# Inverse square roots by one power on GpSimd, and eight weight subtractions moved to VectorE

## The chip, the core and the metric

The kernel runs on one core of a Trainium2 chip. The metric is the time of one execution on the device in microseconds; the time before is the median of three runs.

## What is computed

One inference step of a layer with two kinds of mixer. 512 prompt tokens and 8 sequences of 4 new ("sample") tokens, 1,024 wide, are RMS-normalised and multiplied by one input matrix. Its columns are q and k (4 heads, each twice 64), v (4 x 128), and u and a gate input (512 each) of a gated MLP. Everything that matters here is where an inverse square root stands:

```python
def rms_norm(x, g):
    y = x * lax.rsqrt(jnp.mean(x * x, axis=-1, keepdims=True) + EPS)
    return y * g

z  = rms_norm(x, norm_mix) @ w_in
q  = rms_norm(z[q columns] per head half, q_gain)        # k the same
gv = rms_norm(gelu(z[gate columns]) per group, gv_gain)
mix = gelu(z[u columns]) * (W_s gv + b)                  # W_s lower triangular, 128 x 128
att = softmax(q1 k1) v - lam * softmax(q2 k2) v          # causal; sample tokens also read 4,096 cached rows
h   = x + [rms_norm(att, subln_gain) * 0.8, mix] @ w_out
out = h + relu(rms_norm(h, norm_ffn) @ w_up)**2 @ w_down
```

The outputs are y, k and v for both kinds of token and the sample's gv.

## The kernel before

Exact float32 products are made from split operands: every weight tile of 128 x 1,024 that is loaded (`raw`) is copied by ScalarE into `wh` (float32r), and the rest `raw - wh` goes into `wl`; TensorE then multiplies hi by hi, lo by hi and hi by lo. `w_conv()` does this split. Its subtraction runs on VectorE, except that of weight tiles 12 to 19, which runs on GpSimd:

```python
(G if 12 <= i < 20 else V).tensor_tensor(out=lo, in0=raw, in1=hi, op=ALU.subtract)
```

The stages follow one another on TensorE: a set-up (0 to about 60 us: x is loaded, transposed, split, its own norms `x_stat` taken, and the sample's q heads made), ten passes of `in_proj` over 256 columns each (q, k, v, gate, u, two passes each), the prompt's attention (16 units of one head and 128 queries, woven into `in_proj` from its eleventh half pass on), `out_proj`, and the FFN in eight groups. Beside all of them runs the cache stream: 64 chunks of gathered keys and values (`kraw`, `v`). GpSimd issues the gathers. VectorE's `k_tr(n)` transposes chunk n into `kt`, which frees a buffer of two, and only then is the gather of keys n + 2 written into GpSimd's order; a gather of values follows in the same way once TensorE has used a buffer of three. `S` is the product of `kt` with the sample's queries `qz`.

What order each engine runs in is decided by a scheduler that simulates the program, within bounds: GpSimd keeps exactly the written order, VectorE and TensorE may run 28 places out of it, ScalarE and SyncE freely; during the set-up all keep it (`pinned`). Every instruction goes through one helper, so all of them have line L52 in the profile, and one reads by tiles.

`rsqrt(x, eps, e, mul)` is an estimate from the bits and three Newton steps, eleven small instructions on VectorE or, with `e` given, fourteen on GpSimd. Its calls:

- on GpSimd, in the set-up: `x_stat` for the sample (32 x 1), for prompt tile 0 (128 x 1) and for tiles 1 to 3 (128 x 3), result `rst`, a part of the tile `cst`; and the sample's q heads (`cst`, 32 x 8), after which VectorE multiplies `zn` by `cst`.
- on VectorE: q, k and gate columns in `finish_piece` (`ssb`, 128 x 16, 128 x 20 and 128 x 10, two passes each; for gates the factor goes into `mix<-mix,ssb,gg`); the norm of the attention's output in `attn_c` (128 x 4, a tile `s`, four times); and three in `sample_merge`, `out_proj` and the sample's output.

Small tiles of one to 24 columns all have the name `s`.

Of the kernel before, what the change touches and what calls it, by code (L numbers as in the profile page):

```python
# [19 lines left out]
NCH = 64           # chunks of 128 gathered rows (four keys each): eight per sequence  # L20
# [4 lines left out]
NG = 8             # groups of 512 hidden units  # L25
G1 = 5             # the first group that takes the sample's tokens along
LAG = 11           # chunks between the scores' keys and the values
RAWB = 2           # buffers of weights as loaded
KB = 2             # buffers of gathered keys
VB = 3             # buffers of gathered values  # L30
NPL = 6            # unsplit weights that are loaded ahead
PLX = 2            # and buffers of those in use
WINDOW = 28        # how far VectorE and TensorE may run out of the written order
P_AT = 10          # the slot, after a sequence's first keys, in which its weights are transposed
ATT0 = 11          # the half pass of in_proj with which the prompt's attention starts
ATTW = 2.4         # the weight of the attention's steps against the products' in the stream's pace
D0 = 0.6           # the pace of the stream's first and last slots
# [3 lines left out]
class Ordered:  # L41
    """An engine whose instructions stay within `window` places of the order in which they are written
    (1: exactly that order; 0: no limit)."""
# [19 lines left out]
def kernel(  # L63
# [125 lines left out]
    rst = cst[:, 8:13]  # L189
    rst8 = const.tile([128, 4], F32, name="rst8")  # L190
# [49 lines left out]
    def w_issue(t=None):  # L240
        """Loads the next weights, while there is room; `plain` ones are not split."""
        if st["next"] == len(WL):
            return False
        src, split_it = WL[st["next"]]
        if split_it:
            if t is None:
                if st["issued"] >= st["done"] + RAWB:
                    return False
                t = wp.tile([128, 4, 256], F32, tag="raw", name="raw", bufs=RAWB)
            raws.append(t)  # L250
            st["issued"] += 1
        else:
            if len(plain) >= st["plain"]:
                return False
            t = pools["w"].tile([128, 4, 256], F32, tag="plain", name="plain", bufs=st["plain"] + PLX)
            plain.append(t)
        SP.dma_start(out=t, in_=src)
        st["next"] += 1
        return True

    def w_conv():
        """Splits the next weights exactly: raw = hi + lo, both in float32r."""
        i = st["done"]
        if raws:
            raw = raws.pop(0)
            if i == 3:
                hi, lo = wq[:, 0], wq[:, 1]
            else:
                pool = pools["w"] if i % 5 > 2 else wp
                hi = pool.tile([128, 4, 256], F32R, tag="wh", name="wh")  # L270
                lo = pool.tile([128, 4, 256], F32R, tag="wl", name="wl")
            A.copy(out=hi, in_=raw)
            (G if 12 <= i < 20 else V).tensor_tensor(out=lo, in0=raw, in1=hi, op=ALU.subtract)
            cvt.append((hi, lo))
            st["done"] += 1
            while w_issue():
                pass
# [12 lines left out]
    def later(fn, d=1):  # L290
        """Calls fn in the d-th next flush()."""
        pend[d - 1].append(fn)
# [7 lines left out]
    def rsqrt(x, eps, e=None, mul=None):  # L300
        """x = (x * mul + eps) ** -0.5: a first guess from the bits, then three Newton steps."""
        e = e or V
        n, k = x.shape
        a, b = st_(), st_()
        y, t = a[:n, 0:k], b[:n, 0:k]
        yi = y.bitcast(I32)
        if mul is None:
            e.tensor_scalar(out=x, in0=x, scalar1=eps, scalar2=None, op0=ALU.add)
        else:
            e.tensor_scalar(out=x, in0=x, scalar1=mul, scalar2=eps, op0=ALU.mult, op1=ALU.add)  # L310
        e.tensor_scalar(out=yi, in0=x.bitcast(I32), scalar1=-0.5, scalar2=float(0x5F3759DF), op0=ALU.mult, op1=ALU.add)
        for i in range(3):
            z = x if i == 2 else y
            e.tensor_tensor(out=t, in0=y, in1=y, op=ALU.mult)
            if e is V:
                V.scalar_tensor_tensor(out=t, in0=t, scalar=-0.5, in1=x, op0=ALU.mult, op1=ALU.mult)
                V.scalar_tensor_tensor(out=z, in0=t, scalar=1.5, in1=y, op0=ALU.add, op1=ALU.mult)
            else:
                e.tensor_tensor(out=t, in0=t, in1=x, op=ALU.mult)
                e.tensor_scalar(out=t, in0=t, scalar1=-0.5, scalar2=1.5, op0=ALU.mult, op1=ALU.add)  # L320
                e.tensor_tensor(out=z, in0=t, in1=y, op=ALU.mult)

    def x_stat(t0, srcs, n, junk, e):
        ss = st_()
        m = len(srcs)
        for i, src in enumerate(srcs):
            rms_stat(src, n, ss, 2 * i, junk)
        r = rst[:n, t0:t0 + m]
        sv = ss[:n, 0:2 * m].rearrange("p (m k) -> p m k", k=2)
        e.tensor_tensor(out=r, in0=sv[:, :, 0], in1=sv[:, :, 1], op=ALU.add)  # L330
        rsqrt(r, EPS, e)
        if t0 < 4:
            e.tensor_scalar(out=rst8[:, t0:t0 + m], in0=r, scalar1=SCALE, scalar2=None, op0=ALU.mult)
# [24 lines left out]
    def gelu2(ps, n, g2):  # L358
        """Twice the tanh form of gelu."""
        c = zt_()  # L360
        A.activation(out=c[:n], in_=ps, func=ACTF.Square)
        V.scalar_tensor_tensor(out=c[:n], in0=c[:n], scalar=1.0 / 0.044715, in1=ps, op0=ALU.add, op1=ALU.mult)
        A.activation(out=c[:n], in_=c[:n], func=ACTF.Tanh, scale=0.7978845608028654 * 0.044715)
        V.scalar_tensor_tensor(out=g2, in0=c[:n], scalar=1.0, in1=ps, op0=ALU.add, op1=ALU.mult)
# [30 lines left out]
    # ---------------------------------------------------------------- set-up  # L395
    def pinned(on):
        """Keeps every engine to the written order (on), or within the usual windows."""
        for e in (V, A, PE, G, SP):
            e.window = 1 if on or e is G else WINDOW if e is V or e is PE else 0

    def keep_warm(n):
        """Products that nobody reads: TensorE's clock drops when it idles."""
        ps = dt_()
        for i in range(n):
            mm(ps[:, 0:128], idt, idt, True, True)

    def setup():
# [19 lines left out]

        for t in ssb + [cst]:
# [13 lines left out]
        # functions of the partition index  # L442
# [9 lines left out]
        # sample tokens: transposed, split  # L452
# [10 lines left out]
        # gathered rows  # L463
# [83 lines left out]
    # ---------------------------------------------------------------- cache  # L547
# [23 lines left out]
    def k_tr(n):  # L571
        """Transposes gathered keys in blocks of 32: the feature within its quarter goes to the partitions."""
# [27 lines left out]
    def sm1(b):  # L600
        """The maximum of each row over this partition's keys."""
# [7 lines left out]
    def sm2(b):  # L609
        """The maximum over the rows that share a query, then the weights of the softmax and their sums."""  # L610
# [17 lines left out]
    def ptr(b, k, part):  # L628
        """The softmax weights with the keys on the partitions, as the values lie."""
# [43 lines left out]
    # micro-steps of the cache stream: (time position in slots, function)  # L673
# [31 lines left out]
    def pump(dt):  # L705
        """Gives out the stream's steps that are due after `dt` more of the dense work."""
# [10 lines left out]
    # ---------------------------------------------------------------- dense parts (generators)  # L717
# [16 lines left out]
    def optB(ps, t, hiw, low, half, first=0):  # L734
        """Half the contraction for 128 tokens and 256 columns: hi*hi + hi*lo + lo*hi."""
# [7 lines left out]
    def tr_pair(zn, n, dst, scale):  # L743
        """Transposes two blocks of 128 columns."""
# [89 lines left out]
    def in_proj(gm, F, gsrc, junk):  # L834
# [33 lines left out]
        rsqrt(cst[:32, 0:8], EPS, G)  # L868
# [147 lines left out]
    def attn_c(i, h):  # L1016
# [11 lines left out]
        if h == 3:  # L1028
            rsqrt(ss[:, 0:4], EPS, None, 1.0 / 128.0)
# [7 lines left out]
    def cat_tile(i, k0s=(0, 4)):  # L1037
        """The mixer's output for 128 tokens, transposed and split."""
# [101 lines left out]
    def h_tr(m):  # L1140
        """Rows of the residual stream become columns."""
# [5 lines left out]
    def h_split(m, tok, src):  # L1147
        """The FFN's input before its normalisation, with the gain, in two parts."""
# [88 lines left out]
    def finish(dp):  # L1237
        """Output columns of one pass: the normalisation's factor, squared by the activation, comes in here."""
# [18 lines left out]
    def tiled(ps, lhs, w, first, last):  # L1257
        """Four blocks of the contraction side by side: partitions 32b to 32b + 31 of `ps` get block b."""
# [35 lines left out]
    def sample_merge():  # L1294
        """Joins the softmax over the cache with the one over the new tokens."""
# [122 lines left out]
```

## Time and profile before

| | |
|---|---|
| median of three runs | 854.45 us (854.04 to 855.37) |
| span of the profiled execution | 852.4 us |
| TensorE (PE) busy | 813.6 us, 95% |
| VectorE (DVE) busy | 565.5 us, 66% |
| ScalarE (ACT) busy | 357.2 us, 42% |
| GpSimd (POOL) busy | 183.0 us, 21% |

The profiler records one execution. Its span runs from the first instruction to the last; the median of the timed runs is 2.05 us more than this span, which is what lies around it. TensorE's busy time counts pipelined products, so 95% busy is not 95% of its peak.

### The profile page before, as it was taken

The page shows a single profiled execution, that of the slowest core. Times are in us where ns is not written, and L with a number is a line of the kernel's source. Part 1 is how long each engine was busy: PE and PEld are TensorE (multiplying, and loading weights), DVE is VectorE, ACT ScalarE, POOL GpSimd, SP SyncE. Part 2 cuts the span into 40 slices and gives each one's busy share as a digit, 9 for nine tenths or more (in the row PEclk, how much of TensorE's full clock was granted, in tenths as well). Part 3 has the DMA queues.
Part 4 walks back from the last instruction along what each step waited for, and adds up shares of the span by engine and source line. Part 5 has one row for each costly group of instructions (what it writes and reads, how often), then busy time and mean ns, then how long its engine had stood idle before and what let it go on. Part 6 is the DMA issues. An engine that isn't in the chain of part 4 may idle for free.

```text
span 852.4 us, 15576 instructions
## 1 busy us (share of the span) xinstructions
PE 813.6 (95%) x6210; PEld 630.5 (74%) x6210; DVE 565.5 (66%) x1092; ACT 357.2 (42%) x888; POOL 183.0 (21%) x227
## 2 busy tenths in 40 slices
PE   5898999889899999999999999999999999999997
PEld 4797887656556778876666766655776888999997
DVE  5878976889988884778667586643755544334354
ACT  4543643756465752555144144153233441231231
POOL 6641234234233222112223222221000000000000
PEclk9999999999999999999999999999999999999999
DMA  8586698777868889977889797877298367577302
GB/s 307 188 318 239 234 379 288 278 296 271 325 240 356 281 308 317 332 261 249 327 299 336 298 349 298 303 261 275 75 311 258 105 201 251 179 250 233 100 11 96
DMA packets 101797, 219.07 MB, mean 257 GB/s; under 512 B 6088, under 2 KB 83996, under 8 KB 85340
## 3 DMA queue, kind: packets, MB, share of 16 engines
q0 software_dynamic: 18432, 134.23, 41.8%
q1 hardware_dynamic: 83292, 83.84, 30.7%
q8 instruction: 49, 0.80, 0.4%
q14 instruction: 24, 0.20, 0.1%
HBM read 213.53 MB, written 4.52 MB: 256 GB/s over the span
## 4 chain that ended last, share of the span: by engine, by line
PE 72%; DVE 14%; ACT 6%; DMA 4%; issue 2%; POOL 1%; SPq 1%; DVEq 0%; POOLq 0%
PE d L52 62%; PE O L52 6%; PE S L52 4%; DVE kt L52 4%; DVE s L52 4%; ACT PT L52 3%; DMA kraw<-in_cache_k_dram,idxK 2%; DMA r<-in_x_prompt_dram 1%; DVE wl L52 1%; SPq L52 1%; DMA gg<-in_lambda_q_dram 1%; DVE t L52 1%; ACT t L52 1%; DVE mix L52 1%; ACT z L52 1%
## 5 line engine op out<-in xcount | busy, mean ns | idle before, releaser
L52 ACT CAST wh<-raw 128x1024 fp32r<-128x1024 f32 x90 | 94.2, 1048 | 191.7 <-PE d L52 175.0
L52 PE MATMUL d<-a,wh 128*128 128x272 f32 (+1 forms) x704 | 168.6, 342 | 0.4 <-DVE a L52 0.4
L52 DVE STREAM_TRANSPOSE kt<-kraw 128x2048 f32<-128x2048 f32 x64 | 146.8, 2300 | 14.1 <-PE S L52 7.1
L52 PEld LDWEIGHTS d<-a,wh 128*128 128x128 f32 x704 | 112.8, 188 | 29.5 <-issue 7.1
L52 DVE TENSOR_TENSOR wl<-raw,wh 128x1024 fp32r<-128x1024 f32 x82 | 99.6, 1218 | 50.9 <-ACT wh L52 50.5
L52 PE MATMUL d<-wh,Thi 128*128 128x256 f32 x432 | 128.9, 298 | 2.5 <-ACT d L52 2.5
L52 POOL DMA_INDIRECT v<-in_cache_v_dram,idxK x64 | 70.8, 1106 | 262.6 <-PE O L52 249.4
L52 PE MATMUL d<-wh,Tlo 128*128 128x256 f32 x432 | 123.0, 285 | 1.0 <-DVE Tlo L52 1.0
L52 PE MATMUL d<-wl,Thi 128*128 128x256 f32 x432 | 123.1, 285 | 0.0
L52 PE MATMUL d<-Thi,wh 128*128 128x272 f32 (+2 forms) x368 | 108.9, 338 | 0.0
L52 PE MATMUL d<-Tlo,wh 128*128 128x272 f32 (+2 forms) x368 | 106.3, 331 | 1.9 <-DVE Tlo L52 1.9
L52 PE MATMUL d<-Thi,wl 128*128 128x272 f32 (+2 forms) x368 | 106.1, 330 | 0.0
L52 PE MATMUL d<-a,wl 128*128 128x272 f32 (+1 forms) x352 | 102.8, 336 | 0.0
L52 PEld LDWEIGHTS d<-wh,Thi 128*128 128x128 f32 x432 | 82.4, 191 | 21.2 <-issue 13.9
L52 POOL DMA_INDIRECT kraw<-in_cache_k_dram,idxK x64 | 67.4, 1053 | 117.2 <-DVE kt L52 61.4
L52 PEld LDWEIGHTS d<-wh,Tlo 128*128 128x128 f32 x432 | 82.5, 191 | 2.1 <-DVE Tlo L52 1.2
L52 PEld LDWEIGHTS d<-wl,Thi 128*128 128x128 f32 x432 | 82.3, 190 | 0.1
L52 PEld LDWEIGHTS d<-Thi,wh 128*128 128x128 f32 x368 | 63.6, 189 | 24.2 <-issue 15.0
L52 PE MATMUL O<-v,PT 128*32 128x512 f32 x512 | 73.9, 607 | 2.3 <-ACT PT L52 2.3
L52 ACT COPY PT<-d 32x128 f32<-32x128 f32 x256 | 65.6, 256 | 14.4 <-DVE d L52 10.7
L52 PEld LDWEIGHTS d<-Tlo,wh 128*128 128x128 f32 x368 | 63.9, 189 | 8.4 <-DVE Tlo L52 2.1
L52 PEld LDWEIGHTS d<-Thi,wl 128*128 128x128 f32 x368 | 63.4, 189 | 6.1
(269 smaller groups left out, 1096.0 us busy)
## 6 DMA issues: line engine op xcount, KB each, us to landing
raw<-in_w_up_dram SPq DMA_DIRECT2D x32, 512.0 KB, 4.9
raw<-in_w_down_dram SPq DMA_DIRECT2D x32, 512.0 KB, 4.6
plain<-in_w_up_dram SPq DMA_DIRECT2D x20, 512.0 KB, 4.2
plain<-in_w_down_dram SPq DMA_DIRECT2D x20, 512.0 KB, 5.7
raw<-in_w_in_dram SPq DMA_DIRECT2D x18, 512.0 KB, 7.7
raw<-in_w_out_dram SPq DMA_DIRECT2D x8, 512.0 KB, 6.4
plain<-in_w_out_dram SPq DMA_DIRECT2D x8, 512.0 KB, 8.1
r<-in_x_prompt_dram SPq DMA_DIRECT2D x4, 512.0 KB, 9.1
```

The costliest lines, as they stand in the source:

```text
L52: r = f(*args, **kw)
```

## The change

`rsqrt` loses the engine argument and always runs on GpSimd: one multiply-add where there is an eps or a factor, and one power with an exponent tile `mhalf` of -0.5, which a new memset fills in the set-up. All subtractions of `w_conv` run on VectorE.

```diff
+    mhalf = const.tile([128, 24], F32, name="mhalf")
...
-            (G if 12 <= i < 20 else V).tensor_tensor(out=lo, in0=raw, in1=hi, op=ALU.subtract)
+            V.tensor_tensor(out=lo, in0=raw, in1=hi, op=ALU.subtract)
...
-    def rsqrt(x, eps, e=None, mul=None):
+    def rsqrt(x, eps, mul=1.0):
         n, k = x.shape
...
-        for i in range(3):
-            z = x if i == 2 else y
-            e.tensor_tensor(out=t, in0=y, in1=y, op=ALU.mult)
...
+        if eps or mul != 1.0:
+            G.tensor_scalar(out=x, in0=x, scalar1=mul, scalar2=eps, op0=ALU.mult, op1=ALU.add)
+        G.tensor_tensor(out=x, in0=x, in1=mhalf[:n, 0:k], op=ALU.pow)
...
-        rsqrt(r, EPS, e)
+        rsqrt(r, EPS)
...
+        G.memset(mhalf, -0.5)
...
-        rsqrt(cst[:32, 0:8], EPS, G)
+        rsqrt(cst[:32, 0:8], EPS)
...
-            rsqrt(ss[:, 0:4], EPS, None, 1.0 / 128.0)
+            rsqrt(ss[:, 0:4], EPS, 1.0 / 128.0)
```

What moves on the engines, in three places. On GpSimd in the set-up, the end of the q heads' inverse root (`cst`, 32 x 8), two gathers of keys, and the start of the inverse root for prompt tiles 1 to 3 (128 x 3); before:

```order
L52 TENSOR_TENSOR s<-s 32x8 x2
L52 TENSOR_TENSOR s<-s,cst 32x8
L52 TENSOR_SCALAR s<-s 32x8
L52 TENSOR_TENSOR cst<-s 32x8
L52 DMA kraw<-in_cache_k_dram,idxK 128x2048 x2
L52 TENSOR_TENSOR cst<-s 128x3
L52 TENSOR_SCALAR cst<-cst 128x3
L52 TENSOR_SCALAR s<-cst 128x3
L52 TENSOR_TENSOR s<-s 128x3
L52 TENSOR_TENSOR s<-s,cst 128x3
L52 TENSOR_SCALAR s<-s 128x3
L52 TENSOR_TENSOR s<-s 128x3 x2
```

and now, from the gain of prompt tile 3 (`r<-r,gm`) to the gathers of values:

```order
L52 TENSOR_TENSOR r_87<-r_89,gm 128x1024
L52 TENSOR_SCALAR cst<-cst 32x8
L52 TENSOR_TENSOR cst<-cst,mhalf 32x8
L52 DMA kraw<-in_cache_k_dram,idxK 128x2048 x2
L52 TENSOR_TENSOR cst<-s 128x3
L52 TENSOR_SCALAR cst<-cst 128x3
L52 TENSOR_TENSOR cst<-cst,mhalf 128x3
L52 TENSOR_SCALAR rst_117<-cst 128x3
L52 DMA v<-in_cache_v_dram,idxK 128x2048 x2
```

Of the fourteen instructions of each of these two inverse roots two are left, and the gathers of keys and of values stand that much nearer to the row above them.

On VectorE where the first head's attention output is normalised and the first gate columns are; before (the rows `s<-s 128x4` are the last four of an inverse root's eleven, and `r<-r,s,sg` uses the result):

```order
L52 SCALAR_TENSOR_TENSOR s<-s 128x4
L52 SCALAR_TENSOR_TENSOR mix<-z 128x256
L52 SCALAR_TENSOR_TENSOR t<-t,s 128x256
L52 TENSOR_TENSOR s<-s 128x4
L52 TENSOR_REDUCE s<-d 128x1
L52 SCALAR_TENSOR_TENSOR s<-s 128x4
L52 TENSOR_REDUCE s<-d 128x1
L52 TENSOR_REDUCE ssb_117<-z 128x2
L52 SCALAR_TENSOR_TENSOR s<-s 128x4
L52 TENSOR_SCALAR s<-s 128x2
L52 SCALAR_TENSOR_TENSOR r_87<-r_87,s,sg 128x128 x4
L52 SCALAR_TENSOR_TENSOR z<-z 128x256
```

and now, in twelve rows of the same steps of the attention's units (`s<-d`, `t<-t,s`) that end seven rows ahead of `r<-r,s,sg`:

```order
L52 TENSOR_TENSOR wl<-raw,wh 128x1024
L52 TENSOR_REDUCE s<-d 128x1 x2
L52 SCALAR_TENSOR_TENSOR z<-z 128x256
L52 TENSOR_SCALAR s<-s 128x2
L52 TENSOR_REDUCE s<-d 128x1
L52 TENSOR_TENSOR wl<-raw,wh 128x1024
L52 RECIPROCAL s<-s 128x2
L52 SCALAR_TENSOR_TENSOR mix<-z 128x256
L52 SCALAR_TENSOR_TENSOR s<-s,neglam 128x1
L52 TENSOR_REDUCE s<-d 128x1
L52 SCALAR_TENSOR_TENSOR t<-t,s 128x256
L52 TENSOR_REDUCE ssb_118<-z 128x2
```

The Newton rows between the attention's steps have left the engine, and two subtractions of 128 x 1,024 stand between those steps.

On TensorE in the set-up, where the third pair of key chunks meets the queries (`S<-kt,qz`), behind the last product of a half pass; before:

```order
L52 MATMUL d<-wh,Tlo 128x256
L52 MATMUL d<-wh,spk 64x256
L52 MATMUL d<-wl,spk 64x256
L52 MATMUL d<-wh,spk 64x256
L52 MATMUL d<-wl,spk 64x256
L52 MATMUL d<-wh,spk 64x256
L52 MATMUL d<-wl,spk 64x256
L52 MATMUL d<-wh,spk 64x256
L52 MATMUL d<-wl,spk 64x256
L52 MATMUL S<-kt,qz 32x256 x16
L52 MATMUL d<-wh,Thi 128x256
L52 MATMUL d<-wl,Thi 128x256
```

and now:

```order
L52 MATMUL d<-wh,Tlo 128x256
L52 MATMUL S<-kt,qz 32x256 x16
L52 MATMUL d<-wh,spk 64x256
L52 MATMUL d<-wl,spk 64x256
L52 MATMUL d<-wh,spk 64x256
L52 MATMUL d<-wl,spk 64x256
L52 MATMUL d<-wh,spk 64x256
L52 MATMUL d<-wl,spk 64x256
L52 MATMUL d<-wh,spk 64x256
L52 MATMUL d<-wl,spk 64x256
L52 MATMUL d<-wh,Thi 128x256
L52 MATMUL d<-wl,Thi 128x256
```

The eight products of weights with the packed sample tokens (`spk`) have gone from ahead of `S` to behind it.

## Rows read from the trace of the kernel before

**Rows 1.** The page: busy time of each engine, with its share of the span, and the chain that ended last by engine.

```profile
PE 813.6 (95%) x6210; PEld 630.5 (74%) x6210; DVE 565.5 (66%) x1092; ACT 357.2 (42%) x888; POOL 183.0 (21%) x227
...
PE 72%; DVE 14%; ACT 6%; DMA 4%; issue 2%; POOL 1%; SPq 1%; DVEq 0%; POOLq 0%
```

**Rows 2.** Busy time by stretches: length, busy time of PE, PEld, DVE, ACT and POOL (instructions in brackets), granted TensorE clock, DMA share, GB/s.

```profile
160.00:200.00 40.00, 34.29 (x296) 23.25 (x295) 33.62 (x94) 26.51 (x89) 12.28 (x10) 0.96 0.71 263
200.00:240.00 40.00, 35.08 (x280) 22.18 (x273) 36.63 (x94) 22.10 (x70) 15.09 (x13) 1.00 0.78 276
240.00:280.00 40.00, 39.64 (x328) 25.63 (x327) 35.12 (x79) 22.07 (x64) 14.01 (x12) 1.00 0.88 332
...
65.00:70.00 5.00, 2.74 (x33) 1.29 (x34) 4.42 (x13) 0.00 (x0) 0.94 (x1) 0.84 0.64 229
70.00:75.00 5.00, 5.00 (x36) 5.00 (x37) 4.01 (x8) 1.91 (x5) 0.94 (x1) 0.82 0.55 195
```

**Rows 3.** Timeline of POOL (GpSimd) in the set-up: start, length, instruction, shapes, count, idle time just before it and what ended that.

```profile
14.53 2.00 POOL L52 DMA_INDIRECT kraw<-in_cache_k_dram,idxK  x1 [4.48 <-DVE idxK L52]
...
29.51 0.24 POOL L52 TENSOR_SCALAR cst<-cst 32x8 f32<-32x8 f32 x1
29.84 0.19 POOL L52 TENSOR_SCALAR s<-cst 32x8 int32<-32x8 int32 x1
...
33.11 0.19 POOL L52 TENSOR_TENSOR cst<-s 32x8 f32<-32x8 f32 x1
33.82 1.06 POOL L52 DMA_INDIRECT kraw<-in_cache_k_dram,idxK  x1 [0.52 <-DVE zn L52]
...
39.66 0.20 POOL L52 TENSOR_TENSOR cst<-s 128x3 f32<-128x3 f32 x1
...
44.92 0.24 POOL L52 TENSOR_SCALAR rst<-cst 128x3 f32<-128x3 f32 x1
45.31 1.05 POOL L52 DMA_INDIRECT v<-in_cache_v_dram,idxK  x1 [0.15 <-issue]
...
51.34 0.94 POOL L52 DMA_INDIRECT kraw<-in_cache_k_dram,idxK  x1 [0.30 <-DVE s L52]
```

**Rows 4.** Timeline of DVE (VectorE) in the set-up, the same columns.

```profile
29.47 2.30 DVE L52 STREAM_TRANSPOSE kt<-kraw 128x2048 f32<-128x2048 f32 x1
33.33 0.41 DVE L52 TENSOR_TENSOR zn<-zn,cst 32x256 f32<-32x256 f32 x1 [1.56 <-POOL cst L52]
...
46.81 2.30 DVE L52 STREAM_TRANSPOSE kt<-kraw 128x2048 f32<-128x2048 f32 x1
```

**Rows 5.** The chain of work that ended last, followed through 28 to 75 us: start, length, what.

```profile
51.34 13.54 DMA kraw<-in_cache_k_dram,idxK
64.90 2.31 DVE kt L52
```

**Rows 6.** Timeline of PE (TensorE) in the set-up.

```profile
34.41 0.28 PE L52 MATMUL d<-idt,zn 32*128 32x32 f32 x2 [0.99 <-DVE zn L52]
35.76 0.28 PE L52 MATMUL d<-idt,zn 32*128 32x32 f32 x2 [1.07 <-DVE zn L52]
...
62.72 0.28 PE L52 MATMUL d<-wh,spk 128*64 128x256 f32 x1
...
63.52 0.28 PE L52 MATMUL d<-wl,spk 128*64 128x256 f32 x1
67.26 2.62 PE L52 MATMUL S<-kt,qz 128*32 128x256 f32 x32 [3.47 <-DVE ssb L52]
```

**Rows 7.** The chain that ended last, followed through 139 to 236 us: its shares by engine and tile.

```profile
by line: DVE s L52 25.7%; DVE kt L52 16.0%; ACT PT L52 10.5%; PE d L52 8.4%; ACT t L52 5.5%; DVE mix L52 5.3%; DVE t L52 4.7%; ACT z L52 4.4%; issue 3.3%; DVE ssb L52 2.9%; DVE z L52 2.3%; DVE r L52 2.2%; DVE qz L52 1.9%; DVE d L52 1.4%; AC
```

**Rows 8.** POOL in two places of the prompt's attention.

```profile
144.17 2.38 POOL L52 TENSOR_TENSOR wl<-raw,wh 128x1024 fp32r<-128x1024 f32 x1 [2.41 <-ACT wh L52]
...
212.00 2.37 POOL L52 TENSOR_TENSOR wl<-raw,wh 128x1024 fp32r<-128x1024 f32 x1 [3.14 <-ACT wh L52]
```

**Rows 9.** DVE in the same two places, and two of its small instructions while POOL runs no arithmetic.

```profile
144.49 2.09 DVE L52 TENSOR_SCALAR s<-s 128x2 f32<-128x2 f32 x1
...
178.26 0.15 DVE L52 SCALAR_TENSOR_TENSOR s<-s 128x4 f32<-128x4 f32 x1
...
180.83 0.20 DVE L52 SCALAR_TENSOR_TENSOR s<-s,neglam 128x1 f32<-128x1 f32 x1
...
212.11 2.28 DVE L52 SCALAR_TENSOR_TENSOR s<-s 128x4 f32<-128x4 f32 x1
```

**Rows 10.** Groups of DVE's and POOL's instructions from 139 to 236 us: count, busy time, mean ns of one, idle time before them and what ended it.

```profile
L52 DVE SCALAR_TENSOR_TENSOR s<-s 128x4 f32<-128x4 f32 x12 | 6.0, 496 | 0.1
L52 DVE TENSOR_SCALAR s<-s 128x2 f32<-128x2 f32 x11 | 5.1, 461 | 0.1
...
L52 DVE SCALAR_TENSOR_TENSOR s<-s,neglam 128x1 f32<-128x1 f32 x11 | 3.5, 321 | 0.1
...
L52 DVE TENSOR_TENSOR s<-s 128x10 f32<-128x10 f32 x6 | 1.0, 162 | 0.1
...
L52 POOL TENSOR_TENSOR wl<-raw,wh 128x1024 fp32r<-128x1024 f32 x6 | 14.3, 2381 | 11.5 <-ACT wh L52 11.5
```

**Rows 11.** The two engines' weight subtractions over the whole span, the same columns.

```profile
L52 DVE TENSOR_TENSOR wl<-raw,wh 128x1024 fp32r<-128x1024 f32 x82 | 99.6, 1218 | 50.9 <-ACT wh L52 50.5
...
L52 POOL TENSOR_TENSOR wl<-raw,wh 128x1024 fp32r<-128x1024 f32 x8 | 19.0, 2380 | 15.0 <-ACT wh L52 15.0
```

More of the change, by code (lines that the diff above doesn't have):

```diff
@@ L298, in flush @@
             fn()
-    def rsqrt(x, eps, e=None, mul=None):
-        e = e or V
+    def rsqrt(x, eps, mul=1.0):
         n, k = x.shape
[L304 to L311, printed above, removed]
-        for i in range(3):
-            z = x if i == 2 else y
-            e.tensor_tensor(out=t, in0=y, in1=y, op=ALU.mult)
[L315 to L321, printed above, removed]
+        if eps or mul != 1.0:
+            G.tensor_scalar(out=x, in0=x, scalar1=mul, scalar2=eps, op0=ALU.mult, op1=ALU.add)
+        G.tensor_tensor(out=x, in0=x, in1=mhalf[:n, 0:k], op=ALU.pow)
     def x_stat(t0, srcs, n, junk, e):
```

## The prediction

> **What bounds the kernel now.** The page comes first. TensorE is busy for 95% of the span, and the chain that ended last lies on it for 72%, on VectorE for 14% and on GpSimd for 1% [rows 1]. So only time in which TensorE idles can be won, and the stretches say where that is. Behind the prompt's attention it works 39.64 of 40 us, but in the attention, from 160 to 240 us, 34.29 and 35.08 of 40: 10.6 us are missing, while VectorE works 33.62 and 36.63 [rows 2]. Of the 38.8 us that are missing in the whole span (852.4 - 813.6) another 3.47 us lie in one piece in the set-up [rows 6]. I then read the chain inside the two places. In the attention it stands on VectorE for 62% (25.7% on the small tiles `s`, 16.0% on `kt`, and mix, t, ssb, z, r, qz and d with 20.7%) [rows 7]. In the set-up it goes from GpSimd's small instructions to a gather and through `kt` to TensorE's `S` [rows 3, 5, 6].
>
> **The power.** No row of before has one. From below it is bounded by a small two-input row of GpSimd, 0.20 us for 128x3 [rows 3]; from above by GpSimd's longest arithmetic, 2.38 us for 1,024 columns [rows 11]. It has at most 24 columns, so it is nearer to the first; a power is more arithmetic than a product, and I take 0.5 us. With its multiply-add (0.24 us, and the next row 0.33 us behind its start [rows 3]) an inverse root then costs GpSimd 0.83 us. The q heads' fourteen instructions took it from 29.51 to 33.30 us, 3.79 us [rows 3].
>
> **Set-up, first place: the q heads.** VectorE's `zn` waited 1.56 us for `cst` and began at 33.33 us [rows 4]. Now `cst` is done at 29.51 + 0.83 = 30.34 us, and `zn` begins when VectorE is through with `kt`, at 29.47 + 2.30 = 31.77 us. That is 1.56 us earlier, and TensorE, which waited for both transposes of `zn` (0.99 and 1.07 us) [rows 6], moves up by as much. With a power of up to 1.9 us this is the same.
>
> **Set-up, second place: prompt tiles 1 to 3.** Behind this inverse root stand GpSimd's gathers. It ran from 39.66 to 45.16 us, 5.50 us [rows 3]; now it is 0.20 + 0.24 + 0.50 + 0.24 with three gaps of 0.09, 1.45 us. So the first gather of values starts 4.05 us earlier for this, and 1.5 us for the first place: near 39.7 instead of 45.31 us. The gather of keys 5 took 13.54 us to land, and its `kt` and then `S` ended TensorE's idle time of 3.47 us [rows 5, 6]. Its issue can't move up by all of 5.6 us, since its buffer comes free only with an earlier `kt` (46.81 + 2.30 = 49.11 us against an issue at 51.34 us [rows 3, 4]). That `kt` itself moves up by the 1.56 us, so the issue moves up by about 3.7 us, and if the transfer keeps its length `S` begins at 67.26 - 3.7 = 63.6 us. TensorE's own work ahead of it ends by 62.72 - 1.56 = 61.2 us [rows 6]; a transfer that meets less traffic comes near that. I take the middle, 62.4 us, which is 4.9 us earlier. Of this 1.08 us go back: the eight `spk` products (62.72 to 63.80 us [rows 6]), with which TensorE bridged the wait, now stand behind `S`. That leaves 3.8 us. TensorE's granted clock fell to 0.84 and 0.82 in the 10 us after this idle time began [rows 2]: the two 5 us lost 0.8 and 0.9 us if all of TensorE's work there followed the clock. Without most of the idle time I count 1.0 of it back. Set-up: -4.8 us; bounds 0 (the gather lands no earlier than before, with the first 1.5 us swallowed by it) and -6.7 (3.47 + 1.56 + 1.7).
>
> **The attention, 139 to 236 us.** Three edits meet here, all on VectorE.
> - Two inverse roots of 128x4 and two of 128x10 leave it. Eleven rows of 0.15 or 0.16 us are some 1.8 us for each [rows 9, 10], together -7.2 us.
> - Six of GpSimd's eight subtractions lie here [rows 10]. While one runs, small instructions of VectorE stand still until it ends: GpSimd's at 144.17 us takes 2.38 us and VectorE's row at 144.49 us 2.09; at 212.00 us it is 2.37, and VectorE's row at 212.11 us takes 2.28 [rows 8, 9]. Without that such rows take 0.15 us, and 0.20 with `neglam` [rows 9]. So the means of the groups say what was lost: 12 x (0.496 - 0.155) = 4.1 us, 11 x (0.461 - 0.155) = 3.4 and 11 x (0.321 - 0.20) = 1.3 [rows 10]. That is -8.8 us.
> - The six subtractions come to VectorE at 1.22 us [rows 11]: +7.3 us.
>
> The sum is -8.7 us of VectorE in a stretch where it holds 62% of the chain, so I take 62% of it: **-5.4 us**. The bounds are 0 (ScalarE and TensorE hold the chain as soon as VectorE is faster) and -8.7, which TensorE's 10.6 idle us would allow.
>
> The Trainium skill says in the GPSIMD Engine Reference (§ 8, Key points) that GpSimd shares its SBUF interfaces with VectorE, in contention where VectorE's instruction has two SBUF inputs; the rows at 144 and 212 us agree, though the first is one of a single tensor. By its § 4.1 (Engine selection) two-input work on a tile is about twice as slow on GpSimd; 2.38 against 1.22 us agrees for subtractions. By that rule each power would be some 0.3 us, twice a small row of VectorE, and the sum would change by less than 0.5 us.
>
> **Elsewhere: 0.** The other calls (q and k columns, two more heads, the sample's merge, out_proj) lie where products cover them, as in the 40 us behind the attention with TensorE at 39.64 [rows 2]; if that cover is gone, each is worth at most the 1.8 us that leave VectorE. The first power of all stands ahead of 4.48 us in which GpSimd waits for the row indices [rows 3]. The memset lies ahead of the first transfers. The new multiply-adds wait on GpSimd for VectorE or ScalarE, and the gathers behind them wait too, of values for TensorE's `O` and of keys for `kt`. GpSimd works 12.28 and 15.09 of the two stretches' 40 us, 19.0 us of which over the whole span are subtractions that go away [rows 2, 11], so I price these waits at nothing. If one does hold the queue, a gather starts late by that wait, and a later `kt` and TensorE's `S` with it.
>
> **Sum.** -4.8 - 5.4 = -10.2 us. The profiled execution spans 852.4 us, which becomes 842.2; with the 2.05 us around the span the median goes from 854.45 to **844.2 us**.
>
> **Rivals.**
> - *Set-up alone.* VectorE was late in the attention, but ScalarE's `PT`, `t` and `z` stand in the chain with 20.4% and TensorE's `d` with 8.4% [rows 7]; if they are next as soon as VectorE is lighter, only the set-up's part is left: 854.45 - 4.8 = 849.6 us. What speaks for it is that the subtractions fall between the attention's steps on VectorE, 1.22 us at a time. Against it: they replace stalls of 2.1 to 2.4 us at the same places.
> - *The power is long (slower).* GpSimd may compute it by a routine of several us. The set-up breaks even where the power takes as long as the Newton rows did, about 3.5 us; at 8 us the q heads' `zn` is 38.1 - 33.3 = 4.8 us late and the tiles' factors 4.8 + 3.5 = 8.3 us, and TensorE with them; in the attention each of four calls then holds the gathers for 8 us, and what was gained there is gone. With 4 us more for those the time is 854.45 + 8.3 + 4 = 867 us. Against it: no arithmetic row of GpSimd is longer than 2.4 us, and this one has 1/50 of the columns [rows 11]. For it: nothing in the trace shows a power.
> - *The subtractions bring their waits along (no change).* GpSimd waited 15.0 us for `wh` before its eight subtractions [rows 11]. If VectorE, which keeps to an order within 28 places, has to wait for as much where it is on the chain, 62% of 15.0 = 9.3 us eat the gain: about 853.5 us. Against it: the places at which the subtractions now stand are where `wh` had been ready.
>
> The Trainium skill names a further way to the second rival: by the GPSIMD Engine Reference (§ 2.1, Instruction dispatch) the first call of freshly loaded code on GpSimd costs about 6 us. No row here shows it; paid once, ahead of the 4.48 us of waiting, it would cost some 1.5 us by an estimate from that page, and paid at each call it would be the second rival.
>
> **How the numbers follow.** The forecast has a chance of 0.53, set-up alone 0.19, the waits 0.10, the long power 0.15, other mishaps 0.03. Its own range is 839 us (both terms at their bounds, -6.7 - 8.7 = -15.4) to 849 us (half of each). The range that leaves out 2 in 10 reaches from 838 to 855 us: it takes in the first and third rival and leaves out the second. A measurement of this kernel tells 0.2%, 1.7 us, from no change; so faster is 0.53 + 0.19 = 0.72, same 0.10, slower 0.18.
>
> **What would show it.** GpSimd's power rows on `cst`, `ssb` and `s`: under 1 us each if I am right. `zn` near 31.8 us, the first gather of values near 39.7 us, `S` before 64 us, and no 5 us at a clock of 0.8 behind it. In the attention no small row of VectorE of 1.4 to 2.5 us, and TensorE's 160 to 240 us with some 5 us of idle time instead of 10.6. The prediction is wrong if powers take over 2 us, if the third pair's `S` still waits 3 us for its gather, or if TensorE's idle time there stays with ScalarE as the one waited for.

## The result: 842.06 us, and the profile after

The changed kernel takes 842.06 us (median of four runs, 840.96 to 842.67) against 854.7 us for the kernel before on the same chip, a ratio of 0.985 (0.983 to 0.987). Twice more, on the chips of the second and third group of experiments, it took 842.17 and 842.23 us, 0.984 (0.982 to 0.986) and 0.983 (0.981 to 0.986) of the kernel before. The profiled execution spans 841.0 us, 11.4 us less than that of before. It took 842.67 us, so 1.7 us lie around its span, where I had counted 2.05. One execution of the kernel with the power alone took 1,139 us at a granted clock of 0.73, where all others were at 0.98 or above, and is left out below.

Of the page, the busy times and the chain that ended last, which answer to [rows 1]:

```profile
PE 812.3 (97%) x6210; PEld 630.6 (75%) x6210; DVE 547.7 (65%) x957; ACT 357.9 (43%) x888; POOL 187.0 (22%) x196
...
PE 77%; DVE 8%; ACT 7%; DMA 5%; issue 2%; POOL 1%; SPq 0%; DVEq 0%; POOLq 0%; ACTq 0%
```

TensorE's missing time fell from 38.8 to 28.7 us, and its busy time by 1.3 us. VectorE's share of the chain fell from 14 to 8%. The same stretches as in [rows 2]:

```profile
160.00:200.00 40.00, 38.51 (x317) 27.49 (x317) 37.00 (x78) 27.80 (x91) 16.70 (x16) 1.00 0.80 290
200.00:240.00 40.00, 36.23 (x295) 22.22 (x294) 33.47 (x81) 25.53 (x83) 14.53 (x15) 1.00 0.85 318
...
65.00:70.00 5.00, 5.00 (x59) 4.25 (x52) 2.59 (x3) 0.84 (x2) 3.76 (x3) 1.00 0.63 232
70.00:75.00 5.00, 5.00 (x51) 4.66 (x53) 4.55 (x9) 1.58 (x5) 2.24 (x2) 1.00 0.56 190
```

From 160 to 240 us TensorE now lacks 1.49 + 3.77 = 5.3 us instead of 10.6, and the 10 us from 65 us on, which were at a granted clock of 0.84 and 0.82, are at 1.00. The two other profiles of the changed kernel lack 5.2 and 5.7 us from 160 to 240 us; in both the granted clock from 160 to 200 us is 0.96, as it was before. The first of them:

```profile
160.00:200.00 40.00, 38.38 (x304) 27.11 (x305) 35.73 (x74) 27.58 (x89) 13.61 (x15) 0.96 0.76 277
```

In the attention the chain has left VectorE: its shares from 139 to 228 us, against [rows 7]:

```profile
by line: PE d L52 48.6%; PE S L52 7.9%; PE O L52 7.5%; ACT z L52 5.6%; ACT PT L52 5.5%; issue 5.2%; DVE s L52 3.3%; ACT t L52 3.2%; ACT P L52 2.3%; DVE qz L52 1.9%; DVE d L52 1.7%; ACT d L52 1.3%; DVE z L52 1.2%; DVE r L52 1.2%; DVE mix L52
```

`s` has 3.3% where it had 25.7, `kt` is no longer among the named ones, and TensorE's own products `d` have 48.6% where they had 8.4. VectorE's groups in that stretch, against [rows 10]:

```profile
L52 DVE TENSOR_TENSOR wl<-raw,wh 128x1024 fp32r<-128x1024 f32 x5 | 6.1, 1211 | 0.0
...
L52 DVE SCALAR_TENSOR_TENSOR s<-s,neglam 128x1 f32<-128x1 f32 x11 | 2.3, 211 | 0.1
...
L52 DVE TENSOR_SCALAR s<-s 128x2 f32<-128x2 f32 x10 | 1.8, 179 | 0.0
```

The stalls are gone: a row of 128 x 2 takes 179 ns where the mean was 461, and one with `neglam` 211 where it was 321. Subtractions of 1.21 us stand in their place.

What the prediction could not read off the kernel before is what a power costs. GpSimd's groups, over the whole span:

```profile
L52 POOL TENSOR_TENSOR ssb<-ssb,mhalf 128x20 f32<-128x20 f32 x2 | 7.1, 3566 | 0.2
...
L52 POOL TENSOR_TENSOR s<-s,mhalf 128x4 f32<-128x4 f32 x5 | 5.6, 1112 | 2.6 <-DVE rst L52 2.3
L52 POOL TENSOR_TENSOR ssb<-ssb,mhalf 128x10 f32<-128x10 f32 x2 | 4.0, 1988 | 0.2
...
L52 POOL TENSOR_TENSOR s<-s,mhalf 32x4 f32<-32x4 f32 x1 | 1.0, 1040 | 0.1
...
L52 POOL TENSOR_TENSOR cst<-cst,mhalf 128x1 f32<-128x1 f32 x1 | 0.6, 576 | 0.1
```

A power takes 0.58 us for one column and 3.57 us for twenty: (3.566 - 0.576) / 19 = 0.157 us for each further column. All powers together took 27.8 us.

The set-up, on GpSimd (the gain of prompt tile 3, two of the powers, the first gather of values), on VectorE and on TensorE, against [rows 3], [rows 4] and [rows 6]:

```profile
23.96 2.36 POOL L52 TENSOR_TENSOR r<-r,gm 128x1024 f32<-128x1024 f32 x1
...
31.17 1.68 POOL L52 TENSOR_TENSOR cst<-cst,mhalf 32x8 f32<-32x8 f32 x1
...
41.25 0.89 POOL L52 TENSOR_TENSOR cst<-cst,mhalf 128x3 f32<-128x3 f32 x1
...
42.65 2.15 POOL L52 DMA_INDIRECT v<-in_cache_v_dram,idxK  x1 [0.18 <-issue]
...
23.93 2.43 DVE L52 TENSOR_SCALAR bdm<-fg,pf 32x32 f32<-32x32 f32 x1
...
34.43 0.37 DVE L52 TENSOR_TENSOR zn<-zn,cst 32x256 f32<-32x256 f32 x1
...
64.46 1.93 PE L52 MATMUL S<-kt,qz 128*32 128x256 f32 x32
66.32 0.33 PE L52 MATMUL d<-wh,spk 128*64 128x256 f32 x1
...
70.14 0.28 PE L52 MATMUL d<-wh,spk 128*64 128x256 f32 x1
```

TensorE's third `S` begins at 64.46 us, without the 3.47 us of waiting, and the `spk` products stand behind it. The next such products begin at 70.14 us; before they began 3.5 us later:

```profile
73.65 0.28 PE L52 MATMUL d<-wh,spk 128*64 128x256 f32 x1
```

Each trace holds one execution, and this place varies from one to the next. In the five profiles with the old roots in the set-up (before, and four kernels below) these products begin at 70.35 to 74.61 us; in the six with the power there and the gain of tile 3 on GpSimd they begin at 68.38 to 71.29.

The q heads, however, are later: `zn` is multiplied at 34.43 us instead of 33.33. The row at 23.93 us on VectorE, 32 x 32, took 2.43 us. It stood still beside GpSimd's `r<-r,gm`, which the shorter roots let start at 23.96 instead of 27.03 us. In the two other profiles of the changed kernel `zn` comes at 33.39 and 34.10 us. In the first of these GpSimd's gain runs from 23.99 to 26.36 us, and it is another small row of VectorE that stands still until it ends:

```profile
24.81 1.58 DVE L52 TENSOR_SCALAR maskn<-fg,pf 64x32 f32<-64x32 f32 x1
```

### The profile page after: what moved, and what is told of

It is laid out like the page before. It is cut to its first block, busy times and chain, and to the rows that moved or that the text cites. A ratio compares the mean times of both kernels' runs of the same rounds, so it can differ in the third digit from the quotient of the medians.

```text
span 841.0 us, 15425 instructions
## 1 busy us (share of the span) xinstructions
PE 812.3 (97%) x6210; PEld 630.6 (75%) x6210; DVE 547.7 (65%) x957; ACT 357.9 (43%) x888; POOL 187.0 (22%) x196
## 4 chain that ended last, share of the span: by engine, by line
PE 77%; DVE 8%; ACT 7%; DMA 5%; issue 2%; POOL 1%; SPq 0%; DVEq 0%; POOLq 0%; ACTq 0%
PE d L52 66%; PE O L52 6%; PE S L52 5%; DVE kt L52 3%; ACT PT L52 3%; DMA kraw<-in_cache_k_dram,idxK 2%; DMA raw<-in_w_in_dram 2%; DVE wl L52 1%; ACT wh L52 1%; DMA sg<-in_subln_gain_dram 1%; ACT z L52 1%; DVE s L52 1%; ACT t L52 1%; DVE zn L52 1%; ACT P L52 0%
## 5 line engine op out<-in xcount | busy, mean ns | idle before, releaser
L52 DVE STREAM_TRANSPOSE kt<-kraw 128x2048 f32<-128x2048 f32 x64 | 146.8, 2300 | 13.5 <-PE S L52 7.1
L52 DVE TENSOR_TENSOR wl<-raw,wh 128x1024 fp32r<-128x1024 f32 x90 | 109.3, 1218 | 54.6 <-ACT wh L52 54.2
L52 POOL DMA_INDIRECT v<-in_cache_v_dram,idxK x64 | 72.9, 1139 | 269.8 <-PE O L52 252.2
L52 POOL DMA_INDIRECT kraw<-in_cache_k_dram,idxK x64 | 69.1, 1080 | 104.5 <-DVE kt L52 59.8
```

Of the source, the lines that this page charges most:

```text
L52: r = f(*args, **kw)
```

## The experiments

They ask three things: which of the two parts brings the time, whether the set-up and the attention add up as the prediction's sum has it, and what the power's length costs. All ratios are to the kernel before on the same chip; that kernel's median was 856.25 us for the first group of four runs, 855.29 for the second and 856.39 for the third.

### One part without the other

The power everywhere, the eight subtractions back on GpSimd:

```diff
-            V.tensor_tensor(out=lo, in0=raw, in1=hi, op=ALU.subtract)
+            (G if 12 <= i < 20 else V).tensor_tensor(out=lo, in0=raw, in1=hi, op=ALU.subtract)
```

> The power on GpSimd everywhere, the eight subtractions of weight tiles 12 to 19 back on GpSimd. Theory A (both parts count in the attention, as in the sum of the prediction): TensorE lacks some 7 to 8 us from 160 to 240 us (10.6 before, 5.3 in the changed kernel), VectorE's small rows of 1.4 to 2.5 us are there again, and the time is about 846 to 848 us. Theory B (what the attention gained came from taking the subtractions off GpSimd alone): TensorE lacks about 10 us there, and the time is 850 us or more. Theory C (the Newton rows alone made the attention slow): 842 us, as the changed kernel.

846.22 us (median of five), 0.990 (0.987 to 0.993). The stalls are back: a row of 128 x 2 again takes 0.56 us. TensorE lacks 4.39 us from 160 to 200 us, at a granted clock of 0.87, and 3.33 from 200 to 240, together 7.7. The stretches, and the group from 139 to 232 us:

```profile
160.00:200.00 40.00, 35.61 (x269) 25.22 (x270) 31.41 (x65) 25.35 (x85) 16.77 (x15) 0.87 0.63 238
200.00:240.00 40.00, 36.67 (x309) 22.43 (x307) 35.81 (x86) 23.27 (x75) 19.03 (x17) 1.00 0.93 334
```

```profile
L52 DVE TENSOR_SCALAR s<-s 128x2 f32<-128x2 f32 x10 | 5.5, 555 | 0.1
```

That is theory A. Then the other part alone, the Newton steps kept:

```diff
-            (G if 12 <= i < 20 else V).tensor_tensor(out=lo, in0=raw, in1=hi, op=ALU.subtract)
+            V.tensor_tensor(out=lo, in0=raw, in1=hi, op=ALU.subtract)
```

> The kernel before, with all weight subtractions on VectorE and nothing else changed; Newton steps as before. Theory A: in the attention VectorE loses 8.8 us of stalls and gets 7.3 us of subtractions, so 853 to 854 us, and the set-up as before. Theory B (the stalls were the whole loss there): 847 to 849 us, and TensorE lacks some 5 us from 160 to 240 us. Theory C: 854 us or slower, with TensorE lacking 10 us or more there.

853.48 us, 0.9974 (0.9956 to 0.9992), 2.2 us: theory A in size, but not by its reason. TensorE does lack less from 160 to 200 us (3.19 us instead of 5.71), and then meets a wait of `S` for `qz` that the kernel before has with 1.0 us in all, and not there. Two stretches, and the timelines of TensorE and VectorE around it:

```profile
160.00:200.00 40.00, 36.81 (x316) 24.75 (x315) 34.96 (x96) 28.71 (x97) 9.75 (x9) 1.00 0.71 264
200.00:240.00 40.00, 34.29 (x260) 21.21 (x259) 35.41 (x103) 20.66 (x64) 10.97 (x11) 0.91 0.78 289
```

```profile
229.05 3.64 PE L52 MATMUL S<-kt,qz 128*32 128x256 f32 x32 [5.71 <-DVE qz L52]
...
225.37 0.26 DVE L52 COPY qz<-rows 32x32 f32<-32x32 f32 x2
225.66 0.17 DVE L52 SCALAR_TENSOR_TENSOR ssb<-s 128x10 f32<-128x10 f32 x1
```

`S` waits 5.71 us for `qz`. VectorE's copies into `qz` begin only at 225.37 us, mixed with the Newton rows of the second gate columns (128 x 10). The chain is no measure here: from 139 to 240 us it stands on TensorE in this kernel too (`d` 54.1%, VectorE's `s` 1.9%), and yet little was gained.

By the ratios, of 856 us, both parts together (0.984) bring some 13.5 us, the power alone (0.990) 8.6 and the subtractions alone 2.2. That is 2.7 us more than their sum, but each of the three is uncertain by about 2 us, so the runs don't show that they do more than add up.

### Set-up and attention apart

Power in the set-up only; Newton steps on VectorE for all that was there; all subtractions on VectorE (the function `newton` is the old `rsqrt`):

```diff
-            rsqrt(ss[:, 0:w * len(items)], EPS if kind in "qk" else 4.0 * EPS)
+            newton(ss[:, 0:w * len(items)], EPS if kind in "qk" else 4.0 * EPS)
...
-            rsqrt(ss[:, 0:4], EPS, 1.0 / 128.0)
+            newton(ss[:, 0:4], EPS, None, 1.0 / 128.0)
```

> The power in the set-up only (x_stat and the sample's q heads); all roots that were on VectorE keep their Newton steps there, and all subtractions are on VectorE, so against the kernel with the subtractions alone only the set-up differs. Theory A (the set-up's and the attention's gains are separate and add up): the set-up's 3 to 4 us against that kernel, so 849.5 to 851 us where the kernel before has 854.5, TensorE's idle time from 40 to 80 us near 0.2 us, and 9 us idle from 160 to 240 us. Theory B (the attention gains from the stream's earlier start, too): 846 us or less. Theory C (the set-up's gain is swallowed later): 852 us or more.

852.73 us, 0.998 (0.996 to 1.000): no better than the subtractions alone with 0.997. Theory C. Yet the set-up did gain in the profiled execution. Three stretches, and the late `S` on TensorE's timeline:

```profile
40.00:80.00 40.00, 39.52 (x394) 35.18 (x394) 34.30 (x63) 17.85 (x38) 12.95 (x12) 1.00 0.83 313
...
160.00:200.00 40.00, 38.66 (x279) 26.93 (x279) 32.18 (x92) 23.93 (x80) 8.38 (x9) 0.87 0.67 241
200.00:240.00 40.00, 34.29 (x255) 21.13 (x254) 35.39 (x100) 20.93 (x63) 10.30 (x11) 0.91 0.78 292
```

```profile
228.05 3.64 PE L52 MATMUL S<-kt,qz 128*32 128x256 f32 x32 [5.71 <-DVE qz L52]
```

TensorE lacks 0.5 us from 40 to 80 us, where the kernel before lacked 3.47 at once. The second `spk` products on TensorE's timeline, of this kernel and of the one with the subtractions alone, show its lead:

```profile
68.38 0.28 PE L52 MATMUL d<-wh,spk 128*64 128x256 f32 x1
```

```profile
74.61 0.28 PE L52 MATMUL d<-wh,spk 128*64 128x256 f32 x1
```

It is 6.2 us there, and 1.0 us at the `S` that waits for `qz` (228.05 against 229.05 us). In between its granted clock was 0.87 on average from 160 to 200 us, where the other had 1.00: up to 0.13 x 40 = 5.2 us of TensorE's work, which is as much as was lost. That fits, but in one profiled execution, and a long one (856.40 us, where the median is 852.73): TensorE's 6,210 products were busy for 822.1 us in it and for 812.3 us in the changed kernel. No run here sets the clock, so that it is the cause is not shown.

The opposite, power for the attention's output ("heads": one call for each tile of 128 queries, over its four heads) and the gate columns only:

```diff
-        rsqrt(r, EPS)
+        newton(r, EPS, e)
...
-            rsqrt(ss[:, 0:w * len(items)], EPS if kind in "qk" else 4.0 * EPS)
+            (newton if kind in "qk" else rsqrt)(ss[:, 0:w * len(items)], EPS if kind in "qk" else 4.0 * EPS)
...
-        rsqrt(cst[:32, 0:8], EPS)
+        newton(cst[:32, 0:8], EPS, G)
```

> The power for the attention's output and the gate columns only; Newton steps in the set-up on GpSimd and for q and k on VectorE as before; all subtractions on VectorE. Theory A (separate gains): the set-up as before, with TensorE idle for about 3.5 us from 40 to 80 us, and the attention as in the changed kernel with some 5 us idle from 160 to 240 us; 846 to 848 us where the kernel before has 854.5. Theory B (the attention runs well only behind the shorter set-up): 851 us or more.

844.24 us, 0.987 (0.984 to 0.989), beside 842.17 us for the changed kernel, which went along with the expectation below; behind it stand three stretches of the kernel with the attention's powers:

> The changed kernel once more, so that the three others of this group have it on the same chip. 0.984 to 0.986 of the kernel before.

```profile
40.00:80.00 40.00, 39.17 (x382) 34.49 (x382) 32.99 (x64) 15.80 (x34) 13.45 (x23) 0.98 0.82 304
...
160.00:200.00 40.00, 38.67 (x307) 27.78 (x308) 35.72 (x75) 27.29 (x88) 13.58 (x15) 0.96 0.78 280
200.00:240.00 40.00, 36.23 (x300) 22.69 (x300) 34.62 (x84) 25.01 (x83) 15.29 (x16) 1.00 0.84 314
```

The time is 2 us under theory A's range. The attention is as A has it and as in the changed kernel, 1.33 + 3.77 us missing from 160 to 240 us. The set-up is not: TensorE lacks only 0.83 us from 40 to 80 us, though the roots on GpSimd are the old ones. The gather of keys 5 was issued at 49.98 instead of 51.34 us, and `S` began at 65.73:

```profile
65.73 1.93 PE L52 MATMUL S<-kt,qz 128*32 128x256 f32 x32 [0.83 <-DVE ssb L52]
```

With the same set-up this `S` waits 2.55 and 2.21 us in the two kernels of the next section. So the wait of 3.47 us before was not all the root's. The powers of heads and gates bring 9.3 us over the subtractions alone (0.9974 to 0.9865, of 856); all the others bring 2.1 us more, which the intervals just fail to separate.

### Heads or gates

The power for one of the attention's two kinds of root, each with all subtractions on VectorE: gates only, then heads only, with the line for the other kind calling `newton` and all other roots as in the kernel before.

```diff
-            rsqrt(ss[:, 0:4], EPS, 1.0 / 128.0)
+            newton(ss[:, 0:4], EPS, None, 1.0 / 128.0)
```

> The power for the gate columns only; Newton steps for all other roots, all subtractions on VectorE. In the kernel with the subtractions alone, VectorE's copies into qz at 225 us are mixed with the second gate root's Newton rows, and TensorE's S waits 5.7 us for qz. Theory Q (that wait is why the subtractions alone bring so little): with the gates' rows gone the eight copies stand together, the wait shrinks to 2 us or less, and the time is 846 to 849 us where the kernel before has 855. Theory R (what counts is how many rows VectorE has to do): half of the attention powers' 9 us, 848.5 to 850 us, with the wait for qz still there.

```diff
-            (newton if kind in "qk" else rsqrt)(ss[:, 0:w * len(items)], EPS if kind in "qk" else 4.0 * EPS)
+            newton(ss[:, 0:w * len(items)], EPS if kind in "qk" else 4.0 * EPS)
```

> The power for the attention's output only (128 x 4, four calls); Newton steps for all other roots, all subtractions on VectorE. Theory Q: VectorE's copies into qz stay mixed with the gate's Newton rows, TensorE's S still waits some 5 us for qz, and the time is 851 us or more. Theory R: 848.5 to 850 us.

846.83 us for the gates, 0.990 (0.988 to 0.993), and 848.47 us for the heads, 0.991 (0.988 to 0.994). The same `S` on TensorE's timeline, gates first:

```profile
221.54 1.93 PE L52 MATMUL S<-kt,qz 128*32 128x256 f32 x32 [1.40 <-ACT z L52]
```

```profile
219.99 3.64 PE L52 MATMUL S<-kt,qz 128*32 128x256 f32 x32 [3.44 <-DVE qz L52]
```

For the gates theory Q held: this `S` doesn't wait for `qz`, and the time is within its range. For the heads it held by half: the wait is still there with 3.44 us, but the time is 2.5 us better than Q allowed and at the edge of R's range. (The profile is of the shortest of the six executions, 844.05 us; the longest took 851.00.) So the wait for `qz` is one cost of the Newton rows beside the subtractions, not the only one. Over the subtractions alone the gates' powers bring 6.3 us and the heads' 5.4 (0.9900 and 0.9911 against 0.9974, of 856), each uncertain by some 3 us; both together bring 9.3.

### What the power's length costs

Each power done twice:

```diff
+        scr = st_()
+        G.tensor_tensor(out=scr[:n, 0:k], in0=x, in1=mhalf[:n, 0:k], op=ALU.pow)
         G.tensor_tensor(out=x, in0=x, in1=mhalf[:n, 0:k], op=ALU.pow)
```

> The changed kernel, with each power done twice, the first into a scratch tile that nobody reads. In the changed kernel a power took 0.55 us (32 x 1) to 3.57 us (128 x 20), 27.8 us in all, against the 0.5 us that the prediction took for each. Theory A (the length of a power is covered nearly everywhere; only tiles 1 to 3 of the set-up, 0.9 us, and parts of the attention's 1.1 and 2.0 us lie on the path): 842.5 to 845 us. Theory B (GpSimd's length lies on the path in the set-up and the attention; 1.7 + 0.9 + 2.9 + 2.9 and 1.1 and 2.0 twice each): 848 us or more.

850.76 us, 0.994 (0.992 to 0.996): some 8 us of the 28 that were added are on the path, theory B. The order on VectorE moved too, so a part may be that. TensorE's stretches, and the wait that grew most:

```profile
80.00:120.00 40.00, 36.37 (x327) 30.56 (x326) 27.39 (x59) 23.36 (x68) 23.43 (x14) 1.00 0.67 236
160.00:200.00 40.00, 36.05 (x311) 24.01 (x309) 32.63 (x77) 28.42 (x96) 16.32 (x14) 1.00 0.75 279
200.00:240.00 40.00, 34.93 (x282) 23.91 (x279) 35.17 (x76) 22.34 (x70) 18.84 (x18) 0.96 0.81 299
```

```profile
DVE zn L52 <- POOL ssb L52: 12.3, 2, 7.6
```

From 160 to 240 us TensorE lacks 9.0 us instead of 5.3, as theory B has it. What it did not name are the k columns: two powers of 3.6 us in a row make VectorE wait 12.3 us in two places, and TensorE lacks 3.6 us from 80 to 120 us. In the changed kernel VectorE waits for the single powers there as well, but only 5.6 us:

```profile
DVE zn L52 <- POOL ssb L52: 5.6, 2, 4.0
```

There TensorE lacks only 1.3 us from 80 to 120 us. So once, the long powers are just covered. The next experiment takes them away and makes a second change with it. It has Newton steps for q and k on VectorE again, and the gain of prompt tile 3 on VectorE:

```diff
-        (G if t == 3 else V).tensor_tensor(out=xg[t % 2], in0=xt[t], in1=gm, op=ALU.mult)
+        V.tensor_tensor(out=xg[t % 2], in0=xt[t], in1=gm, op=ALU.mult)
...
-            rsqrt(ss[:, 0:w * len(items)], EPS if kind in "qk" else 4.0 * EPS)
+            (newton if kind in "qk" else rsqrt)(ss[:, 0:w * len(items)], EPS if kind in "qk" else 4.0 * EPS)
```

> The changed kernel with the gain of prompt tile 3 on VectorE, and the roots of q and k (128 x 16 and 128 x 20, whose powers take 2.9 and 3.6 us against eleven rows of 0.17 us) back as Newton steps on VectorE. If the long powers cost anything in the changed kernel: 839 to 840.5 us. If products cover them, and VectorE's rows too: 841 to 842 us. If VectorE's 8 us more are on the path: 843 us or more.

841.13 us, 0.984 (0.982 to 0.986), where the changed kernel beside it took 842.17: the middle case. But the gain of tile 3 alone, in the next section, gives 0.982. Against that the Newton rows cost 1 to 2 us, with overlapping intervals. So products cover either form to within some 2 us; which is better isn't shown.

### The stall that moved into the set-up

The gain of prompt tile 3 alone on VectorE, the first line of the diff above; run in the first and, beside the changed kernel, in the third group.

> The changed kernel, with the gain of prompt tile 3 (r<-r,gm, 128 x 1,024) on VectorE instead of GpSimd. In the changed kernel GpSimd ran it from 23.96 to 26.32 us, and a row of VectorE (bdm, 23.93 us) took 2.43 us instead of 0.22, ahead of Tlo and the q heads; TensorE's transposes of zn came 1 us later than before instead of 1.6 us earlier. Theory A (that stall made the q heads late): the bdm row takes 0.2 us, VectorE gets 1.2 us in its place, zn is some 1 us earlier or more, and the time is 840 to 841.5 us. Theory B (the weights' and tiles' loads set the pace there): zn no earlier, 842 us or slower.

> The changed kernel with the gain of prompt tile 3 on VectorE once more, beside the changed kernel on one chip. If its 0.9824 was real: 1 to 2 us less than the changed kernel. If the set-up's microseconds are given back later, as those of the power in the set-up were: no difference that the interval shows.

> The changed kernel, on the chip of this group: 0.984 to 0.985 of the kernel before, some 841 to 842.5 us.

841.67 us, 0.982 (0.980 to 0.985), and 840.48 us, 0.982 (0.980 to 0.984); the changed kernel beside the second 842.23 us, 0.983 (0.981 to 0.986). VectorE's timeline with the gain on it:

```profile
23.69 1.21 DVE L52 TENSOR_TENSOR r<-r,gm 128x1024 f32<-128x1024 f32 x1
...
25.16 0.22 DVE L52 TENSOR_SCALAR bdm<-fg,pf 32x32 f32<-32x32 f32 x1
...
32.37 0.37 DVE L52 TENSOR_TENSOR zn<-zn,cst 32x256 f32<-32x256 f32 x1
```

The 32 x 32 row takes 0.22 us again, and `zn` comes at 32.37 us (32.48 in the second run), 0.9 to 2.1 us earlier than in the three profiles of the changed kernel. So the stall was the cause of the late q heads. The first time lies just above theory A's range. In the third group 1.75 us at the median are left at the end, with overlapping intervals: probably a little faster than the changed kernel, and the fastest that was run.

## Why the prediction was right, point by point

The time lies 2.1 us under the 844.2 forecast, in the range, by the mechanism that carried the larger term. Several of its steps were mis-sized or failed and partly made up for each other, so that it came this close is in part luck.

- **The power, 0.5 us.** Failed. It took 0.54 to 3.57 us, above the bound of 2.38 us that I had from GpSimd's subtraction of 1,024 columns, and over the 2 us that I had named as a sign of being wrong. A row of another operation, however long, bounds nothing here, since a power costs 0.157 us a column beside 0.42. What saved the sum was that the wide ones (q and k) lie under TensorE's products, and that GpSimd waits anyway; doubled, they cost 8 us. The slow rival was nearer than I took it to be: with powers twice as long over half of the gain is gone.
- **q heads, 1.56 us earlier.** Failed in sign: 1.10 us later (0.1 and 0.8 in the two other profiles). The rule of the stalls stood in my own rows, and I applied it to the eight subtractions only. GpSimd has one more instruction of that width, the gain of tile 3, and the shorter root ahead of it moved it by 3.1 us onto VectorE's path. Taken off GpSimd, `zn` came to 32.37 us.
- **Tiles 1 to 3 and the third `S`.** The first gather of values came at 42.65 us, not 39.7: the q heads are 2.5 us of it (1.0 later instead of 1.5 earlier) and the power 0.4. `S` began at 64.46 instead of 62.4. The idle 3.47 us and the low clock went, as forecast; the set-up's gain in the profiled execution was 3.5 instead of 4.8 us by the second `spk` products. But with the old roots and the attention's powers they began at 70.55 us, only 0.4 us later. So a part of the 3.5 us is not the root's, and how much stays open.
- **Set-up and attention add up.** Failed. The set-up's power alone brings nothing that can be told (0.998 against 0.997), and without it, and without the other powers outside the attention, the kernel loses 2.1 of 13 us. The sum was made of terms that the runs don't find apart.
- **The attention, -5.4 us.** Right in kind, too small: 9.3 us for the powers of heads and gates plus 2.2 for the subtractions. The 62% of 8.7 us counted VectorE's rows, and TensorE's missing time from 160 to 240 us fell by just that 5.4 us (10.6 to 5.3). The gain beyond that isn't settled. The granted clock from 160 to 200 us doesn't explain it: it is 1.00 in one profile of the changed kernel and 0.96 in two, as before [rows 2]. In the kernel with the attention's powers, 2.6 of the 3.5 us that TensorE lacked from 40 to 80 us are gone, and that is ahead of the attention. The wait of `S` for `qz`, 5.7 us with the subtractions alone and 1.5 us in the changed kernel, was in no sum of mine. And VectorE's share of the chain was a poor price for its rows, since with the subtractions alone the chain left VectorE and only 2.2 us were gained.
- **Rivals.** The set-up alone fell: ScalarE did not hold the attention. The subtractions did not bring their waits along: VectorE's idle time ahead of all its subtractions, in the page's group, is 54.6 us where it was 50.9 [rows 11], 3.7 us more and not the 15.0 of the third rival. In the sum of the long power, 38.1 us should be 29.51 + 0.33 + 8 = 37.8.

```profile
L52 DVE TENSOR_TENSOR wl<-raw,wh 128x1024 fp32r<-128x1024 f32 x90 | 109.3, 1218 | 54.6 <-ACT wh L52 54.2
```

The sentence in which the Trainium skill's GPSIMD Engine Reference (§ 2.1, Instruction dispatch) puts about 6 us on the first call of freshly loaded code has no counterpart here: the first power of all, at 5.07 us, began 0.08 us after the row ahead of it had ended and took 0.55 us, as much as the later one of one column.

## What to carry to other kernels

A long instruction that stalls a neighbour is best taken away along with the neighbour's many short rows: here the long instructions alone brought 2.2 us, since behind them the short rows made a new wait (`S` for `qz`), and both brought 13.5. When an instruction is shortened, look at what starts earlier behind it, and at what that meets on other engines. A stage's gain can be gone by the end, as that of the set-up's power was, so measure it with the other stages changed and unchanged. A trace is one execution: before a microsecond in it is put down to an edit, look at the same place in the other profiles of the same code.

## What the hardware showed that I had not expected

- GpSimd's power costs by columns and not by partitions: 1.04 us for 32 x 4 and a mean of 1.11 us for 128 x 4. With 0.157 us for a column it is as long per column as a whole small product row of VectorE.
- It doesn't stall VectorE as the wide subtraction does. While a power of 128 x 10 ran on GpSimd, VectorE's small rows took what they take alone (timelines of the changed kernel):

```profile
211.65 1.99 POOL L52 TENSOR_TENSOR ssb<-ssb,mhalf 128x10 f32<-128x10 f32 x1
...
212.28 0.18 DVE L52 SCALAR_TENSOR_TENSOR s<-s,neglam 128x1 f32<-128x1 f32 x1
...
213.03 0.15 DVE L52 TENSOR_SCALAR mc<-mc 128x1 f32<-128x1 f32 x1
```

- GpSimd's own small rows were held by VectorE's wide ones in turn, in two places. The multiply-add of the first tile's heads took 0.91 us at 170.35 us instead of 0.19, beside VectorE's subtraction that ran from 169.99 to 171.21 us; a sum of 128 x 1 took 1.15 us at 21.57 us instead of 0.19, beside VectorE's gains of tiles 1 and 2, which ran until 22.67.
